# Regrouping the 512- and 256-column matmuls of a feed-forward block, and a 64-row contraction widened to 128 rows

## The chip, the cores and the metric

The kernel runs on one core of a Trainium2 chip. The metric is the device time of one execution in microseconds (us): the median of several runs. Beside it, one execution was taken with the hardware profiler, and its trace is what the rows below are copied from.

## The reference: what is computed

One decoder layer in float32 on 256 tokens of width 2048, then a final RMSNorm. Cut to its outline:

```python
h = rmsnorm(x, attn_norm_g)
proj = h @ w_in                         # split into latent q, latent kv, a shared rotary key, NSA q/k/v, gates
o_mla = mla_group(...)                  # 8 heads: s = q_nope.k_nope + q_rope.k_rope, causal softmax, p @ v
o_nsa = nsa_group(...)                  # 16 heads: compressed, selected and window branches, ALiBi, gates
x = x + concat(o_mla, o_nsa) @ w_o
h = rmsnorm(x, ffn_norm_g)
x = x + (silu(h @ w_gate) * (h @ w_up)) @ w_down      # D_FF = 5632
out = rmsnorm(x, final_norm_g)
```

Two places matter here. One is `h @ w_gate` and `h @ w_up`, which are 2048 x 5632 each. The other is the rotary term of the MLA scores, `q_rope . k_rope`, which contracts over 64 numbers per head.

## The kernel before, in words

**Numbers in two parts.** TensorE takes its operands in a reduced float32 form, so every operand is split into a high part (a rounded copy) and a low part (what the rounding left), and a product a·b is made as hi·hi + hi·lo + lo·hi. A weight chunk of 128 x 1024 float32 numbers is brought by a DMA (`wraw`), ScalarE writes its high part (`whi`, line 143) and VectorE its low part (`wlo`, line 145). `Stream` does this for all chunks in one fixed order: the DMA of a chunk is issued three chunks ahead and its split two ahead, in rings of three buffers. On SyncE's queue these DMAs stand in the order of the program, and each waits until its buffer is free.

**Order of the work.** TensorE's order is written out by hand in `program()`: the input projection, the NSA heads with other projections between them, the eight MLA heads with chunks of the output projection between them, the rest of the output projection, then the feed-forward block in two halves. The order on the other engines and queues comes from a scheduler that simulates the program.

**Gate and up.** A half is 22 tiles of 128 feed-forward columns. Each tile takes two weight chunks of `w_gate` and two of `w_up`; a chunk holds eight 128 x 128 pieces, one for each of eight groups of 128 inputs. The weights are the stationary operand, and the moving operand is `h2T`, the normed input transposed, with its high and low part side by side (2 x 256 columns). For each piece, `mmA` (line 212) issues two matmuls into one PSUM bank:

```python
nc.tensor.matmul(ps[0:hi.shape[1], :], hi, act, start=start, stop=False)                   # L214: 512 columns
nc.tensor.matmul(ps[0:hi.shape[1], 0:S], lo, act[:, 0, :], start=False, stop=stop)         # L215: 256 columns
```

`gate_up` (line 789) calls it for the eight pieces of a chunk, so on TensorE a 512-column matmul and a 256-column one take turns, each with a weight load of its own. There are 704 such pairs in each half (2 matrices, 22 tiles, 16 pieces), 1408 in all. When both chunks of a tile's `up` are done, `activate` (line 817) takes the two banks. Between and after the two halves, `down` multiplies by `w_down` with 512-column matmuls alone (lines 858 to 860), 528 in a half.

**The rotary key.** `rope_key` (line 576) makes the rotated key and splits it. Its high part `KRH` is stored twice, on partitions 0 to 63 and 64 to 127; so is its low part `KRL` (line 545, 128 x 256). A head's rotary query `qr[:, hh]` holds the query's high part on one half of the partitions and its low part on the other, so one matmul over 128 rows (line 615) gives (hi + lo)·KRH. The low part of the key is multiplied by the query's high half alone, with 64 rows (line 616):

```python
hr = slice(64 * hh, 64 * hh + 64)
nc.tensor.matmul(sv, qr[:, hh, q_], KRH[:, 0:n], start=False, stop=False)
nc.tensor.matmul(sv, qr[hr, hh, q_], KRL[hr, 0:n], start=False, stop=False)
```

`mla_scores` (line 605) does this twice in each of eight heads, for 128 and for 256 key columns, and follows it with the causal mask, a bf16 matmul by an identity (line 617). The NSA scores have a similar chain (lines 445 to 452), with a contraction over 70 rows, and the product of the NSA probabilities with the values (lines 516 and 517) is a run of two 512-column and two 256-column matmuls.

Of the kernel before, what the change touches and what calls it, by code (L numbers as in the profile page):

```python
# [9 lines left out]
F32 = mybir.dt.float32  # L10
F32R = mybir.dt.float32r
# [5 lines left out]
P = 128  # L17
S = 256
D = 2048
KD = D // P  # L20
# [140 lines left out]
def layer_kernel(ctx: ExitStack, tc: tile.TileContext, a: dict, out: bass.AP):  # L161
    nc = tc.nc
# [43 lines left out]
    def bcast_rows(dst, col, ps):  # L206
# [1 line left out]
        for t in range(2):  # L208
            nc.tensor.transpose(ps[:, t * P:(t + 1) * P], col[:, t:t + 1].to_broadcast([P, P]), ident)
        nc.scalar.copy(dst, ps[:, 0:S])  # L210

    def mmA(ps, hi, lo, act, start, stop):

        nc.tensor.matmul(ps[0:hi.shape[1], :], hi, act, start=start, stop=False)  # L214
        nc.tensor.matmul(ps[0:hi.shape[1], 0:S], lo, act[:, 0, :], start=False, stop=stop)  # L215

    def mm3(ps, hi, lo, act, start, stop):

# [4 lines left out]
    ps = ctx.enter_context(tc.tile_pool(name="ps", bufs=1, space=bass.MemoryType.PSUM))  # L223

    def bank(tag, name):
        return ps.tile([P, 512], F32, tag=tag, name=name, bufs=2 if tag in ("ds", "PT") else 1)
# [8 lines left out]
    ap = att.enter_context(tc.tile_pool(name="att", bufs=1))  # L235
# [32 lines left out]
    for k in range(KD):  # L268
        if k in (0, 1, 6, 10):
            c0 = (k + 3) // 4 * 4 if k < 6 else k + 2  # L270
            t = xcs[c0] = ap.tile([P, 4, S], F32, tag="xt", name=f"xt{c0}", bufs=2)
# [13 lines left out]
        if k in (5, 7, 9, 11):  # L285
            i = (k - 5) // 2
            t, xs = i // 2, slice(i % 2 * 1024, i % 2 * 1024 + 1024)
# [19 lines left out]
        hi, lo = W.get(("g1", k))  # L307
        st, sp = k == 0, k == KD - 1
# [74 lines left out]
    st = {}  # L383
# [158 lines left out]
    ckvT = ap.tile([P, 2, 2, S], F32R, tag="xt", name="ckvT", bufs=2)  # L542
    sqs = ap.tile([P, 2, S], F32, tag="xt", name="sqs", bufs=2)
    KRH = ap.tile([P, S], F32R, name="KRH")
    KRL = ap.tile([P, S], F32R, name="KRL")

    QR = oT[:, 4:8]

    def split(dh, dl, u, eng=nc.vector):
        nc.scalar.copy(dh, u)  # L550
        eng.tensor_sub(dl, u, dh.bitcast(F32))
# [24 lines left out]
    def rope_key():  # L576
        rp = bank("S0", "ps_ropek")
        nc.tensor.matmul(rp[0:64, 0:S], perm[0:64, 0:64], krg[0:64], start=True, stop=True)
        t = ap.tile([P, S], F32, tag="u", name="rt_k", bufs=2)
        nc.vector.tensor_mul(t[0:64], rp[0:64, 0:S], sinT[0:64])  # L580
        nc.gpsimd.tensor_mul(krg[0:64], krg[0:64], cosT[0:64])
        nc.gpsimd.tensor_add(t[0:64], krg[0:64], t[0:64])
        split(KRH[0:64], KRL[0:64], t[0:64])
        nc.scalar.copy(KRH[64:128], KRH[0:64].bitcast(F32))
        nc.vector.tensor_copy(KRL[64:128], KRL[0:64].bitcast(F32))

    def rope_queries(j):

# [16 lines left out]
    def mla_scores(m):  # L605
        hh, qn, qr = m % 2, st["qn", m], QR[:, m // 2]
        sb = bank("S0", f"ms_{m}")
        hr = slice(64 * hh, 64 * hh + 64)
        for t, sv in ((0, sb[:, 0:P]), (1, sb[:, P:384])):
            q_ = slice(t * P, (t + 1) * P)  # L610
            n = (t + 1) * P
            nc.tensor.matmul(sv, qn[:, 0, q_], KN[:, m, 0, 0:n], start=True, stop=False)
            nc.tensor.matmul(sv, qn[:, 0, q_], KN[:, m, 1, 0:n], start=False, stop=False)
            nc.tensor.matmul(sv, qn[:, 1, q_], KN[:, m, 0, 0:n], start=False, stop=False)
            nc.tensor.matmul(sv, qr[:, hh, q_], KRH[:, 0:n], start=False, stop=False)
            nc.tensor.matmul(sv, qr[hr, hh, q_], KRL[hr, 0:n], start=False, stop=False)
            nc.tensor.matmul(sv[:, n - P:n], identb, maskb[:, 0, :], start=False, stop=True)
        nm = ap.tile([P, 2, 2], F32, tag="nm", name=f"mnm{m}", bufs=2)
        ls = ap.tile([P, 2, 2], F32, tag="ls", name=f"mls{m}", bufs=2)
        nc.vector.tensor_reduce(nm[:, 0, 0:1], sb[:, 0:P], axis=AX.X, op=ALU.max)  # L620
        nc.vector.tensor_reduce(nm[:, 0, 1:2], sb[:, P:384], axis=AX.X, op=ALU.max)
        nc.vector.tensor_scalar(nm[:, 0, :], nm[:, 0, :], -MLA_SCALE, None, op0=ALU.mult)
        e = ap.tile([P, 768], F32, tag="e", name=f"me{m}", bufs=4)
        for t, c in ((0, slice(0, P)), (1, slice(P, 384))):
            nc.scalar.activation(e[:, c], sb[:, c], AF.Exp, bias=nm[:, 0, t:t + 1], scale=MLA_SCALE,
                                 accum_out=ls[:, 0, t:t + 1])
        nc.vector.reciprocal(ls[:, 0, :], ls[:, 0, :])
        for t, c in ((0, slice(0, P)), (1, slice(P, 384))):
            nc.vector.tensor_scalar(e[:, c], e[:, c], ls[:, 0, t:t + 1], None, op0=ALU.mult)
        st["me", m] = e  # L630
# [129 lines left out]
    for step in steps:  # L760
        op, args = step[0], step[1:]
        if op == "w":
            key = args[0]
            n = key[0]
            if n == "gate":
                break
            if n == "uk" and KN is None:
                big = hp.tile([P, KD, 2, S], F32R, tag="big", name="kn_v")
                KN = big[:, 0:8]
                VMM = big[:, 8:16].rearrange("p (t s a) h c -> p t s (a h c)", t=2, s=2)  # L770
            if n == "woM" and h2T is None:
                h2T = hp.tile([P, KD, 2, S], F32R, tag="big", name="h2T")
            w = W.get(key)
            if n in ("q", "cq", "ckv"):
                w_in_block(key, w)
            elif n in ("w1k", "w1v"):
                compress_hidden(n[2], key[1], w)
            elif n in ("woN", "woM"):
                w_o(key, w)
            else:  # L780
                {"uk": w_uk, "uv": w_uv, "uq": w_uq}[n](key[1], w)
        else:
            {"gates": do_gates, "rope_k": rope_key, "ck": compress_keys, "cv": compress_values,
             "ssq": latent_sum, "rb": latent_rows, "rope": rope_queries, "qk": nsa_scores, "t": nsa_transpose,
             "pv": nsa_pv, "tc": cmp_transpose, "pvc": cmp_pv, "mqk": mla_scores, "mt": mla_transpose,
             "mpv": mla_pv, "tp": transpose_x}[op](*args)


    def gate_up(key, w):
        n, f, j = key  # L790
        hi, lo = w
        if j == 0:
            st[n, f] = bank("ds" if n == "gate" else "PT", f"{n}{f}")
        for kk in range(8):
            k, c = 8 * j + kk, slice(kk * P, (kk + 1) * P)
            mmA(st[n, f], hi[:, c], lo[:, c], h2T[:, k], k == 0, k == KD - 1)

    W.share = 0
    while step[0] == "w":
        gate_up(step[1], W.get(step[1]))  # L800
        step = next(steps)
# [29 lines left out]
    for h in range(2):  # L831
        done = 0
        while done < NFH:
            step = next(steps)
            if step[0] == "rb2":
                bcast_rows(RB, rstd[:, 3, :], bank2("ps_rb2")[:, 0, :])
                continue
            n, f, j = step[1]
            gate_up(step[1], W.get(step[1]))
            if (n, j) == ("up", 1):  # L840
                activate(h, f - h * NFH)
                done += 1
# [179 lines left out]
```

## Time and profile before

| | us |
|---|---|
| median of 3 runs | 1085.76 |
| lowest, highest | 1083.0, 1086.45 |
| the profiled execution | 1083.73 |
| its span, first to last instruction | 1081.9 |
| TensorE busy in the span | 1059.7 |
| VectorE, ScalarE, GpSimd busy | 643.8, 563.3, 205.1 |

"Busy" TensorE counts modelled durations that overlap, so it can't be read as time at full rate. How fast the matmuls really follow each other is read from their start times: the difference between two starts, or a stretch between two starts divided by the number of matmuls in it.

### The profile page before, as it was taken

What the parts mean: (1) busy time and instruction counts of PE and PEld (TensorE: products, weight loads), DVE (VectorE), ACT (ScalarE), POOL (GpSimd) and SP (SyncE); (2) the same over time, 40 slices, a digit from 0 to 9 for tenths busy, and PEclk for the clock granted to TensorE, in tenths of its full rate; (3) what the DMA queues carried; (4) which work ended last, traced back from release to release, by engine and by line L of the source; (5) the groups of instructions that cost most, each with busy time, mean ns of one, the idle gap of its engine ahead of it and who ended that gap; (6) DMA issues with size and microseconds to landing.
All of it is one profiled execution on the core that took longest, in us unless ns stands there. A gap on an engine that the chain in (4) does not pass through costs nothing.

```text
span 1081.9 us, 16205 instructions
## 1 busy us (share of the span) xinstructions
PE 1059.7 (98%) x6102; PEld 926.0 (86%) x6102; DVE 643.8 (60%) x1017; ACT 563.3 (52%) x994; POOL 205.1 (19%) x206
## 2 busy tenths in 40 slices
PE   8999998999999999999999999999999999999996
PEld 8999997878888888888888888888888888888885
DVE  5568889885556555555555444455555555555554
ACT  6648887854455554544454333345444454444442
POOL 2234445533342100101010000001010010101110
PEclk9999999999999999999999999999999999999999
DMA  8845432334456555555565566655555555555653
GB/s 282 283 134 182 136 119 98 101 98 134 134 176 215 184 188 192 191 186 188 193 194 186 192 194 192 193 192 185 186 190 182 192 181 190 186 186 194 193 195 136
DMA packets 54831, 193.57 MB, mean 179 GB/s; under 512 B 6436, under 2 KB 6948, under 8 KB 54624
## 3 DMA queue, kind: packets, MB, share of 16 engines
q1 hardware_dynamic: 54288, 191.36, 53.9%
q0 software_dynamic: 464, 1.17, 0.3%
q8 instruction: 48, 0.79, 0.3%
q14 instruction: 31, 0.25, 0.1%
HBM read 190.41 MB, written 2.10 MB: 178 GB/s over the span
## 4 chain that ended last, share of the span: by engine, by line
PE 87%; DVE 4%; DMA 4%; ACT 2%; issue 2%; POOL 0%; SPq 0%; DVEq 0%; POOLq 0%; ACTq 0%
PE up L214 15%; PE gate L214 15%; PE gate L215 8%; PE up L215 8%; PE dn L859 7%; PE dn L858 7%; PE dn L860 7%; DMA wraw<-in_g_dram 2%; DMA wraw<-in_w_dram 1%; PE woM L747 1%; PE woM L748 1%; PE woM L749 1%; PE ps_q L219 1%; PE ps_q L220 1%; PE ps_q L221 1%
## 5 line engine op out<-in xcount | busy, mean ns | idle before, releaser
L145 DVE TENSOR_TENSOR wlo<-wraw,whi 128x1024 fp32r<-128x1024 f32 (+3 forms) x352 | 416.6, 1184 | 388.8 <-ACT whi L143 387.8
L143 ACT CAST whi<-wraw 128x1024 fp32r<-128x1024 f32 (+2 forms) x352 | 366.4, 1041 | 450.0 <-PE dn L860 125.1
L214 PE MATMUL gate<-h2T,whi 128*128 128x512 f32 x704 | 248.7, 395 | 0.0
L214 PE MATMUL up<-h2T,whi 128*128 128x512 f32 x704 | 248.5, 395 | 0.0
L215 PE MATMUL gate<-h2T,wlo 128*128 128x256 f32 x704 | 197.4, 280 | 0.0
L215 PE MATMUL up<-h2T,wlo 128*128 128x256 f32 x704 | 197.4, 280 | 0.0
L826 POOL TENSOR_TENSOR u<-t,RB 128x512 f32<-128x512 f32 x44 | 57.1, 1297 | 556.6 <-DVE t L825 556.6
L214 PEld LDWEIGHTS up<-h2T,whi 128*128 128x128 f32 x704 | 132.0, 187 | 31.0
L214 PEld LDWEIGHTS gate<-h2T,whi 128*128 128x128 f32 x704 | 132.0, 187 | 31.0
L858 PE MATMUL dn<-whi,aT 128*128 128x512 f32 x352 | 137.0, 389 | 0.0
L860 PE MATMUL dn<-whi,aT 128*128 128x512 f32 x352 | 137.0, 389 | 0.0
L859 PE MATMUL dn<-wlo,aT 128*128 128x512 f32 x352 | 137.0, 389 | 0.0
L215 PEld LDWEIGHTS gate<-h2T,wlo 128*128 128x128 f32 x704 | 133.0, 189 | 0.1
L215 PEld LDWEIGHTS up<-h2T,wlo 128*128 128x128 f32 x704 | 133.0, 189 | 0.0
L147 POOL TENSOR_TENSOR wlo<-wraw,whi 128x256 fp32r<-128x256 f32 x70 | 89.2, 1275 | 145.5 <-ACT whi L143 122.9
L858 PEld LDWEIGHTS dn<-whi,aT 128*128 128x128 f32 x352 | 66.1, 188 | 13.9
L860 PEld LDWEIGHTS dn<-whi,aT 128*128 128x128 f32 x352 | 66.1, 188 | 13.8
L859 PEld LDWEIGHTS dn<-wlo,aT 128*128 128x128 f32 x352 | 66.1, 188 | 13.5
L219 PE MATMUL ps_q<-hT,whi 128*128 128x256 f32 x128 | 38.1, 298 | 2.2 <-ACT RB L210 2.2
L221 PE MATMUL ps_q<-hT,wlo 128*128 128x256 f32 x128 | 36.9, 288 | 0.0
L220 PE MATMUL ps_q<-hT,whi 128*128 128x256 f32 x128 | 36.8, 288 | 0.0
L219 PEld LDWEIGHTS ps_q<-hT,whi 128*128 128x128 f32 x128 | 25.3, 198 | 2.9 <-ACT RB L210 2.5
(322 smaller groups left out, 1489.2 us busy)
## 6 DMA issues: line engine op xcount, KB each, us to landing
wraw<-in_w_dram SPq DMA_DIRECT2D x338, 512.0 KB, 3.5
wraw<-in_g_dram SPq DMA_DIRECT2D x14, 440.0 KB, 5.0
x<-in_x_dram SPq DMA_DIRECT2D x4, 512.0 KB, 5.9
out_dram<-x SPq DMA_DIRECT2D x8, 256.0 KB, 2.6
xt<-in_xT_dram SPq DMA_DIRECT2D x3, 512.0 KB, 6.2
gfin<-in_gfin_dram POOLq DMA_DIRECT2D x1, 1024.0 KB, 5.9
wraw<-in_g_dram SPq DMA_DIRECT2D x2, 256.0 KB, 4.0
wraw<-in_g_dram SPq DMA_DIRECT2D x2, 184.0 KB, 3.3
```

Of the source, the lines that this page charges most:

```text
L143: nc.scalar.copy(hi[:, c0:c1], raw[:, c0:c1])
L145: nc.vector.tensor_sub(lo[:, c0:c2], raw[:, c0:c2], hi[:, c0:c2].bitcast(F32))
L147: nc.gpsimd.tensor_sub(lo[:, c2:c1], raw[:, c2:c1], hi[:, c2:c1].bitcast(F32))
L214: nc.tensor.matmul(ps[0:hi.shape[1], :], hi, act, start=start, stop=False)
L215: nc.tensor.matmul(ps[0:hi.shape[1], 0:S], lo, act[:, 0, :], start=False, stop=stop)
L219: nc.tensor.matmul(ps, hi, act[:, 0, :], start=start, stop=False)
L220: nc.tensor.matmul(ps, hi, act[:, 1, :], start=False, stop=False)
L221: nc.tensor.matmul(ps, lo, act[:, 0, :], start=False, stop=stop)
L826: nc.gpsimd.tensor_mul(u, t2, RB[:, None, :].to_broadcast([P, 2, S]))
L858: nc.tensor.matmul(pts[t], h_, wh, start=f == 0, stop=False)
L859: nc.tensor.matmul(pts[t], h_, wl, start=False, stop=False)
L860: nc.tensor.matmul(pts[t], l_, wh, start=False, stop=f == NFH - 1)
```

## The change

In `gate_up` the pieces of a chunk are taken two at a time: the 512-column matmuls of both come first, then their two 256-column ones. The products, their operands and the bank are the same. In the MLA scores, `KRL` becomes a tile of 128 x 2 x 256 that is filled with zeros at the start of the program; slot 0 has the key's low part on partitions 0 to 63 and zeros on the others, slot 1 has zeros on 0 to 63 and the low part on 64 to 127. The matmul of line 616 takes the slot of its head and runs over all 128 rows, with zeros where the query's low part stands.

```diff
-    def mmA(ps, hi, lo, act, start, stop):
-
-        nc.tensor.matmul(ps[0:hi.shape[1], :], hi, act, start=start, stop=False)
-        nc.tensor.matmul(ps[0:hi.shape[1], 0:S], lo, act[:, 0, :], start=False, stop=stop)
...
-    KRL = ap.tile([P, S], F32R, name="KRL")
+
+    KRL = ap.tile([P, 2, S], F32R, name="KRL")
+    nc.gpsimd.memset(KRL.bitcast(F32), 0.0)
...
-        split(KRH[0:64], KRL[0:64], t[0:64])
+        split(KRH[0:64], KRL[0:64, 0, :], t[0:64])
         nc.scalar.copy(KRH[64:128], KRH[0:64].bitcast(F32))
-        nc.vector.tensor_copy(KRL[64:128], KRL[0:64].bitcast(F32))
+        nc.vector.tensor_copy(KRL[64:128, 1, :], KRL[0:64, 0, :].bitcast(F32))
...
-        hr = slice(64 * hh, 64 * hh + 64)
...
-            nc.tensor.matmul(sv, qr[hr, hh, q_], KRL[hr, 0:n], start=False, stop=False)
+            nc.tensor.matmul(sv, qr[:, hh, q_], KRL[:, hh, 0:n], start=False, stop=False)
...
-        for kk in range(8):
-            k, c = 8 * j + kk, slice(kk * P, (kk + 1) * P)
-            mmA(st[n, f], hi[:, c], lo[:, c], h2T[:, k], k == 0, k == KD - 1)
+        pt = st[n, f]
+        for k2 in range(0, 8, 2):
+            for kk in (k2, k2 + 1):
+                k = 8 * j + kk
+                nc.tensor.matmul(pt, hi[:, kk * P:(kk + 1) * P], h2T[:, k], start=k == 0, stop=False)
+            for kk in (k2, k2 + 1):
+                k = 8 * j + kk
+                nc.tensor.matmul(pt[:, 0:S], lo[:, kk * P:(kk + 1) * P], h2T[:, k, 0, :], start=False, stop=k == KD - 1)
```

On TensorE, the first chunk of the first gate tile stood like this before:

```order
L748 MATMUL woM_4097<-wlo_4150,oT 128x512
L749 MATMUL woM_4097<-whi_4149,oT 128x512
L214 MATMUL gate_4197<-h2T,whi_4168 128x512
L215 MATMUL gate_4197<-h2T,wlo_4169 128x256
L214 MATMUL gate_4197<-h2T,whi_4168 128x512
L215 MATMUL gate_4197<-h2T,wlo_4169 128x256
L214 MATMUL gate_4197<-h2T,whi_4168 128x512
L215 MATMUL gate_4197<-h2T,wlo_4169 128x256
```

and stands like this now (x2 means two alike in a row):

```order
L794 MATMUL gate_4198<-h2T,whi_4169 128x512 x2
L797 MATMUL gate_4198<-h2T,wlo_4170 128x256 x2
L794 MATMUL gate_4198<-h2T,whi_4169 128x512 x2
L797 MATMUL gate_4198<-h2T,wlo_4170 128x256 x2
L794 MATMUL gate_4198<-h2T,whi_4169 128x512 x2
```

The matmuls are the same ones; in each four, the second and the third have changed places.

The scheduler's order of the other engines moves as well. On SyncE's queue, in the input projection's first microseconds (`xt` is the transposed input in pieces of four groups, `wraw` the weight chunks):

```order
 L122 DMA wraw_115<-in_g_dram 128x880
 L122 DMA wraw_155<-in_g_dram 128x880
-L280 DMA xt_150<-in_xT_dram 128x1024
 L122 DMA wraw_184<-in_g_dram 128x880
+L275 DMA xt_150<-in_xT_dram 128x1024
 L122 DMA wraw_215<-in_g_dram 128x880
```

The second piece of the transposed input is now issued behind the fifth weight chunk. ScalarE and VectorE split that chunk before they scale that input piece, where it was the other way round. On GpSimd one memset, that of `KRL`, stands behind the other memsets of the start. In the first half, ScalarE and VectorE now split a tile's result (`aT`) before they read the next tile's gate bank, where it was the other way round.

## Rows read from the trace of the kernel before

**Rows 1.** The page: TensorE's busy time, and the chain that ended last, by line.

```profile
PE 1059.7 (98%) x6102; PEld 926.0 (86%) x6102; DVE 643.8 (60%) x1017; ACT 563.3 (52%) x994; POOL 205.1 (19%) x206
...
PE up L214 15%; PE gate L214 15%; PE gate L215 8%; PE up L215 8%; PE dn L859 7%; PE dn L858 7%; PE dn L860 7%; DMA wraw<-in_g_dram 2%; DMA wraw<-in_w_dram 1%; PE woM L747 1%; PE woM L748 1%; PE woM L749 1%; PE ps_q L219 1%; PE ps_q L220 1%; PE ps_q L221 1%
```

**Rows 2.** Timeline of PE: start, duration (us), instruction, [idle before]; where feed-forward stretches meet.

```profile
352.07 0.48 PE L214 MATMUL gate<-h2T,whi 128*128 128x512 f32 x1
...
585.12 0.39 PE L858 MATMUL dn<-whi,aT 128*128 128x512 f32 x1
...
953.57 0.40 PE L858 MATMUL dn<-whi,aT 128*128 128x512 f32 x1
```

**Rows 3.** Timeline of PE: the first gate matmuls of the second half.

```profile
704.84 0.39 PE L214 MATMUL gate<-h2T,whi 128*128 128x512 f32 x1
705.07 0.28 PE L215 MATMUL gate<-h2T,wlo 128*128 128x256 f32 x1
705.18 0.40 PE L214 MATMUL gate<-h2T,whi 128*128 128x512 f32 x1
```

**Rows 4.** Timeline of PE: first and last of 15 256-column matmuls in a row.

```profile
162.01 0.28 PE L219 MATMUL ps_q<-hT,whi 128*128 128x256 f32 x1
...
163.69 0.28 PE L221 MATMUL ps_q<-hT,wlo 128*128 128x256 f32 x1
```

**Rows 5.** Timeline of PE: NSA probabilities by values, behind the run of rows 4.

```profile
163.81 0.39 PE L516 MATMUL o<-ph,V 128*128 128x512 f32 x1
164.04 0.40 PE L517 MATMUL o<-pl,V 128*128 128x512 f32 x1
164.27 0.29 PE L516 MATMUL o<-ph,V 128*128 128x256 f32 x1
164.40 0.28 PE L517 MATMUL o<-pl,V 128*128 128x256 f32 x1
164.52 0.40 PE L529 MATMUL o<-PCT,VCS 80*128 80x512 f32 x1
```

**Rows 6.** Timeline of PE: score matmuls of the third MLA head (rows*columns of weights first).

```profile
239.56 0.27 PE L614 MATMUL ms<-kn_v,qn 128*128 128x128 f32 x1
239.67 0.27 PE L615 MATMUL ms<-KRH,oT 128*128 128x128 f32 x1
239.87 0.32 PE L616 MATMUL ms<-KRL,oT 64*128 64x128 f32 x1
240.13 0.23 PE L617 MATMUL ms<-maskb,identb 128*128 128x128 bf16 x1
...
240.60 0.28 PE L615 MATMUL ms<-KRH,oT 128*128 128x256 f32 x1
240.81 0.38 PE L616 MATMUL ms<-KRL,oT 64*128 64x256 f32 x1
241.12 0.23 PE L617 MATMUL ms<-maskb,identb 128*128 128x128 bf16 x1
```

**Rows 7.** Timeline of PE: an NSA score's 70-row matmul and the bf16 mask behind it.

```profile
160.69 0.28 PE L451 MATMUL s<-KA,qa 70*128 70x256 f32 x1
160.82 0.29 PE L452 MATMUL s<-maskb,identb 128*128 128x256 bf16 x1
```

**Rows 8.** Busy time by window: window, its length, each engine's busy us, granted clock.

```profile
205.00:240.00 35.00, 33.70 (x205) 27.89 (x203) 29.46 (x66) 21.27 (x51) 11.67 (x11) 1.00 0.30 98
```

**Rows 9.** Timeline of several engines in the first microseconds.

```profile
2.55 0.54 POOL L329 MEMSET bl_k<- 128x512 f32 x1
...
7.16 0.43 SPq L280 DMA_DIRECT2D xt<-in_xT_dram  x1
9.58 0.33 SPq L122 DMA_DIRECT2D wraw<-in_g_dram  x1
...
13.40 1.71 ACT L303 ACTIVATE hT<-xt,gcols 128x256 fp32r<-128x256 f32 x4 [0.33 <-DMA xt<-in_xT_dram]
...
17.07 0.28 PE L219 MATMUL ps_kc<-hT,whi 128*128 128x256 f32 x1
```

## The prediction

> **What bounds the kernel now.** I read the page first. TensorE is busy for 98% of the span, and the chain that ended last runs through its matmuls: gate and up alone hold 46% of it, the large ones 30% and the small ones 16% [rows 1]. A change in the spacing of these matmuls therefore goes straight into the time, unless another engine is late; so all that matters is how far apart matmuls start, which the timeline of PE shows.
>
> Three spacings are worked out from start times. (a) `down` alone: 528 matmuls of 512 columns between 585.12 and 704.84 [rows 2, 3], 226.7 ns each. Half of that, 113.3 ns, is what 256 columns would take at the same rate. (b) 256-column matmuls alone: 14 steps in 1.68 us [rows 4], 120 ns each, so a short matmul costs some 7 ns over its share. Each has a weight load of its own, which must fit beside one short matmul. (c) Gate and up, a pair of 512 and 256 columns: the first half has 672 pairs from 352.07 to 585.12 [rows 2], 346.8 ns each. That is (a) + (b), 226.7 + 120 = 346.7. The second half has 704 pairs from 704.84 to 953.57 [rows 2, 3], 353.3 ns each: the same instructions, 6.5 ns more for every pair. The reader is to see that the alternating order has two steady rhythms, and that the slower one costs 704 x 6.5 = 4.6 us here. The second half came out of `down` with the first pair at 0.34 us (704.84 to 705.18), so nothing was late when it fell into the slow rhythm. Over both halves the mean is (233.05 + 248.73) / 1376 = 350.1 ns a pair, 700 ns for two pairs. The 32 pairs ahead of 352.07 stand between transposes and are taken at this mean.
>
> **The change, gate and up.** No matmul, load, byte or wait is added. Two pairs (large, small, large, small) become a group (large, large, small, small); there are 704 groups. In a group the second large matmul's load and the first small one's load lie under large matmuls; the loads of the second small one and of the next large one lie under short ones. That is two loads under short matmuls in a group, as before in two pairs. What should change is the rhythm: each group has a 512 to 512 step, which in (a) takes 226.7 with nothing left over.
> - Lower bound: everything hidden, 3 x 226.7 = 680 ns a group. Gain (700 - 680) x 704 = 14.1 us.
> - Upper bound: the one stretch of the trace with just this order, two 512s and two 256s on the NSA values, takes 164.52 - 163.81 = 0.71 us [rows 5]. It stands once, behind a run of short matmuls, and its moving operand lies in two pieces. Loss (710 - 700) x 704 = 7.0 us.
> - Taken: 226.7 + 226.7 + 120 + 120 = 693.4 ns, (a) and (b) added up, because that sum is what the first half's pairs hold for 233 us, and a long steady stretch says more of 704 groups than a single four. Gain: (353.3 - 346.7) x 704 = 4.6 us in the second half, nothing in the first, 0.1 us in the 32 pairs: **4.7 us**.
>
> One rule of the Trainium skill speaks against this part. Its page "TensorE: Matmul & The Clock Gate", section LDWEIGHTS, has a load of 128 columns at 106.7 ns, and its section Back-to-back issue gap has 256 columns at 109 ns: by it every load hides under a short matmul too, either order takes the same, and the sum would hold the rotary part alone. The trace does not agree fully: 120 ns against 113.3 [rows 4, 2, 3]. I keep the rule as a rival.
>
> **The change, rotary key.** 16 matmuls lose their 64-row shape. In the third head the step from the 128-row matmul to the 64-row one is 0.20 us where two 128-row ones are 0.11 apart, and the next step, to the mask, is 0.26; for 256 columns the two are 0.21 and 0.31 [rows 6]. Each is long enough for the matmul ahead to run dry before the next weights are loaded. With 128 rows the steps become 0.11 (239.56 to 239.67) and 0.11 for 128 columns; for 256 columns 0.12 by (b), and 0.13 for the step into a bf16 mask, which a 70-row contraction has without such a gap [rows 7]. Saved in a head: (0.20 - 0.11) + (0.26 - 0.11) + (0.21 - 0.12) + (0.31 - 0.13) = 0.51 us, and 4.1 us in eight. The first heads lie in a stretch in which TensorE waits (33.70 us busy of 35, at a granted clock of 1.00 [rows 8]), so one head's gain is put down as lost in waits: **3.6 us** from seven. The bounds are 0 (the steps come from something else) and 4.1.
>
> The Trainium skill has a rule for either side of this. Its page "TensorEngine Tiling (Array Packing)", Key Properties, says that changing the tiling mode drains TensorE, by which the gain is as above. The Trainium skill's "TensorE: Matmul & The Clock Gate", Step-by-step, says that a load takes no less for fewer rows, by which alone the widening would be worth nothing. The steps of 0.20 and 0.26 agree with the first.
>
> **What is moved beside it, costed at nothing.** The second input piece's DMA goes from 7.16 us to just behind the weight DMA at 9.58, so it is issued some 2.8 us later; its first user on ScalarE started at 13.40, and the input group that it brings is first multiplied at 17.07 [rows 9]. Its high part takes 0.43 us (a quarter of 1.71), the low part about as much (an estimate): 2.8 us of slack against 2.8. Cost 0; without cover, at most a few tenths. The memset on GpSimd (0.54 us, as for `bl_k` [rows 9]) stands ahead of a one-column copy that this DMA waits for, and is done long before 9.58. The exchanged readings of the gate banks have a whole tile's time before the bank is used again. A chunk's high part is released by its last large matmul, now one small matmul earlier; its low part at the same place.
>
> **Sum.** 1083.73 (the profiled execution, span 1081.9) - 4.7 - 3.6 = **1075.4 us**. The median of the runs shown is 2.0 us above the profiled execution; more tiles in the slow rhythm could account for that, and it would go with it. It takes some 0.3%, 3.3 us, to tell a run of this kernel from no change.
>
> **The rivals.**
> 1. *The order is indifferent*: the excess belongs to the number of short matmuls, and the rhythm is picked by chance at the start of a half. For it: both rhythms occur with the same code. Against it: the slow one lasts a whole half, so it is no chance from tile to tile. With the present mean the gate and up part is worth nothing, 1083.73 - 3.6 = 1080.1; with 353.3 in both halves the first loses 672 x 6.5 = 4.4 us, 1084.5. The rule of the Trainium skill on load and gap would have it so, without saying which rhythm.
> 2. *The large pair covers more*: it lets the weight path run ahead, so that only one short matmul of a group pays its 7 ns: 226.7 x 2 + 113.3 + 120 = 686.7, a gain of 9.4 us, 1070.7; with all hidden 1066.0. For it: the first small matmul behind `down` was followed after 0.11 us [rows 3]. Against it: it may just hand the delay on.
> 3. *Slower*: two loads in a row under short matmuls leave the weight path behind, and the next large one starts late each time, as in the NSA values: 0.71 us a group gives 1083.73 + 7.0 - 3.6 = 1087.1, and 0.73, if each of those steps is 0.005 worse than shown, 1101. It is slower from 710 ns on. For it: the one example. Against it: long runs of short matmuls hold 120.
> 4. *The rotary gain does not show* (the gap is not the 64 rows', or VectorE's softmax is late instead): 1083.73 - 4.7 = 1079.0.
>
> **How the numbers follow.** Forecast 41%; rival 1 29%, of which a third at 1080.1 counts as faster and the rest as no change; rival 2 17%; rival 3 6%; rival 4 7%. Faster: 0.41 + 0.17 + 0.07 + 0.09 = 0.74; same 0.20; slower 0.06. The range, 1069.5 to 1084.5, leaves out rival 3, the end of rival 2 with all hidden, and a little of rival 1. The forecast's own range is 1074 to 1078.
>
> **What would show it.** In the changed profile: 704.8 us shifted earlier by about 3.6 us and not more; each half of gate and up with groups of 693 ns, some 244 us for 704 pairs; no step of 0.2 us around the line that multiplies by `KRL`; the 64*128 shape gone. Wrong would be: groups at 700 or 707 ns (rival 1), at 687 or less (rival 2), or a wait of TensorE for ScalarE, VectorE or a DMA that is not there now.

## The result and the profile after

| | before | changed |
|---|---|---|
| median of 4 runs, us | 1085.32 | 1077.12 |
| lowest, highest | 1083.0, 1086.45 | 1076.86, 1078.08 |
| the profiled execution | 1083.73 | 1077.04 |
| its span | 1081.9 | 1075.3 |

The changed kernel is faster: a ratio of 0.9934, 95% interval 0.9921 to 0.9947, a small gain of 0.7%. The profiled executions differ by 6.7 us, the medians by 8.2. (The kernel before has one run more here than in its first table.)

On the page of the changed kernel TensorE is still what bounds it, and gate and up still hold 46% of the chain, now under lines 794 and 797 [rows 1].

```profile
PE 1052.0 (98%) x6102; PEld 920.3 (86%) x6102; DVE 645.7 (60%) x1017; ACT 562.9 (52%) x994; POOL 205.5 (19%) x207
...
PE up L794 15%; PE gate L794 15%; PE up L797 8%; PE gate L797 8%; PE dn L860 7%; PE dn L861 7%; PE dn L859 7%; DMA wraw<-in_g_dram 2%; PE ps_q L214 1%; PE woM L743 1%; PE woM L745 1%; PE woM L744 1%; PE ps_q L215 1%; PE ps_q L216 1%; DVE wlo L145 1%
```

The timeline of PE in the changed kernel (start, duration in us, instruction; x2 joins two alike) has these rows at the joints that rows 2, 3 and 6 show of the kernel before: the last matmul of the NSA scores, the third MLA head, the first gate tile, the gate tile behind the transposes, the start of the second half and each start of `down`.

```profile
203.00 0.29 PE L447 MATMUL s<-maskb,identb 128*128 128x256 bf16 x1
...
237.62 0.27 PE L610 MATMUL ms<-kn_v,qn 128*128 128x128 f32 x1
237.73 0.27 PE L611 MATMUL ms<-KRH,oT 128*128 128x128 f32 x1
237.84 0.27 PE L612 MATMUL ms<-KRL,oT 128*128 128x128 f32 x1
237.95 0.23 PE L613 MATMUL ms<-maskb,identb 128*128 128x128 bf16 x1
237.99 0.36 PE L608 MATMUL ms<-kn_v,qn 128*128 128x256 f32 x1
238.20 0.28 PE L609 MATMUL ms<-kn_v,qn 128*128 128x256 f32 x1
...
238.43 0.28 PE L611 MATMUL ms<-KRH,oT 128*128 128x256 f32 x1
238.55 0.28 PE L612 MATMUL ms<-KRL,oT 128*128 128x256 f32 x1
238.67 0.23 PE L613 MATMUL ms<-maskb,identb 128*128 128x128 bf16 x1
...
334.87 0.62 PE L794 MATMUL gate<-h2T,whi 128*128 128x512 f32 x2
...
347.02 0.48 PE L794 MATMUL gate<-h2T,whi 128*128 128x512 f32 x1
...
581.19 0.40 PE L859 MATMUL dn<-whi,aT 128*128 128x512 f32 x1
...
700.88 0.62 PE L794 MATMUL gate<-h2T,whi 128*128 128x512 f32 x2
...
946.10 0.40 PE L859 MATMUL dn<-whi,aT 128*128 128x512 f32 x1
```

The last matmul of the NSA scores and the first gate matmul of the kernel before, on the same view:

```profile
204.59 0.29 PE L452 MATMUL s<-maskb,identb 128*128 128x256 bf16 x1
...
339.86 0.39 PE L214 MATMUL gate<-h2T,whi 128*128 128x512 f32 x1
```

From starts alone, the span divides into six stretches:

| stretch | before, us | changed, us | difference |
|---|---|---|---|
| start to the last matmul of the NSA scores | 204.59 | 203.00 | -1.59 |
| from there to the first gate matmul (the eight MLA heads and the output projection) | 135.27 | 131.87 | -3.40 |
| gate and up, first half | 245.26 | 246.32 | +1.06 |
| `down`, first half | 119.72 | 119.69 | -0.03 |
| gate and up, second half | 248.73 | 245.22 | -3.51 |
| the rest | 128.4 | 129.2 | +0.8 |
| span | 1081.9 | 1075.3 | -6.7 |

The last two differences are taken before rounding.

The reader is to see three things. The long steps around `KRL` are gone: four steps of 0.11, 0.11, 0.12 and 0.12 us stand where rows 6 had 0.20, 0.26, 0.21 and 0.31. A group of four takes 245.22 / 352 = 696.6 ns in the second half, and both halves now have one and the same spacing: 348.5 ns a pair from 347.02 to 581.19 (672 pairs), 348.3 from 700.88 to 946.10 (704), where it was 346.8 and 353.3 [rows 2, 3]. So the second half gained and **the first half lost 1.06 us**. And two stretches in which the prediction put nothing moved, by -1.59 and +0.8.

In the first of these two, the granted clock fell at different places in the two executions. One place is in the NSA queries, where TensorE waits for the copy of `RB` (line 210). The timeline of PE before ([idle before] in brackets):

```profile
49.25 0.39 PE L219 MATMUL ps_q<-hT,whi 128*128 128x256 f32 x1 [2.24 <-ACT RB L210]
...
49.72 0.41 PE L219 MATMUL ps_q<-hT,whi 128*128 128x256 f32 x1
...
52.92 0.36 PE L219 MATMUL ps_q<-hT,whi 128*128 128x256 f32 x1
```

and changed:

```profile
48.87 0.38 PE L214 MATMUL ps_q<-hT,whi 128*128 128x256 f32 x1 [1.64 <-ACT RB L210]
```

TensorE's busy time by window (window, its length, busy us and instructions, granted clock, DMA share, GB/s), before:

```profile
49.60:53.00 3.40, 3.40 (x19) 0.51 0.74 261
189.40:192.80 3.40, 3.40 (x10) 0.53 0.29 81
```

Changed:

```profile
49.60:53.00 3.40, 3.40 (x31) 1.00 0.86 240
70.20:73.60 3.40, 3.40 (x19) 0.57 0.66 210
```

Before, the wait of 2.24 us was followed by a granted clock of 0.51, the level of 1.2 GHz, and 15 matmuls of 256 columns started 0.213 us apart (3.20 us from 49.72 to 52.92) instead of 0.12, which is 1.4 us more. In the changed kernel the clock stayed at 1.00 there, the 2.4 GHz level, and fell near 70 us instead; the kernel before had a second fall near 190 us, which the changed one had not. One fall more in the kernel before, at some 1.4 us (an estimate from the first), is about the 1.59; the waits of this stretch differ too and were not taken apart. Whether this belongs to the change is asked of the repeated runs below.

The second is a wait at the end, where TensorE waits 0.6 us for the split of a chunk of `w_down`. Behind it stands ScalarE, which splits the last chunks, on its timeline in the changed kernel:

```profile
1053.77 2.00 ACT L143 CAST whi<-wraw 128x1024 fp32r<-128x1024 f32 x2 [3.04 <-DMA wraw<-in_w_dram]
```

The same cast in the kernel before:

```profile
1060.30 2.00 ACT L143 CAST whi<-wraw 128x1024 fp32r<-128x1024 f32 x2 [2.05 <-DMA wraw<-in_w_dram]
```

ScalarE waits 3.04 us for the DMA there against 2.05, and only the longer wait reaches TensorE.

### The profile page after: what moved, and what is told of

Read it like the earlier page. It is cut to its first block, busy times and chain, and to the rows that moved or that the text cites. A ratio compares the mean times of both kernels' runs of the same rounds, so it can differ in the third digit from the quotient of the medians.

```text
span 1075.3 us, 16205 instructions
## 1 busy us (share of the span) xinstructions
PE 1052.0 (98%) x6102; PEld 920.3 (86%) x6102; DVE 645.7 (60%) x1017; ACT 562.9 (52%) x994; POOL 205.5 (19%) x207
## 4 chain that ended last, share of the span: by engine, by line
PE 88%; DVE 4%; DMA 4%; ACT 2%; issue 1%; SPq 0%; POOL 0%; DVEq 0%; POOLq 0%; ACTq 0%
PE up L794 15%; PE gate L794 15%; PE up L797 8%; PE gate L797 8%; PE dn L860 7%; PE dn L861 7%; PE dn L859 7%; DMA wraw<-in_g_dram 2%; PE ps_q L214 1%; PE woM L743 1%; PE woM L745 1%; PE woM L744 1%; PE ps_q L215 1%; PE ps_q L216 1%; DVE wlo L145 1%
## 5 line engine op out<-in xcount | busy, mean ns | idle before, releaser
L794 PE MATMUL gate<-h2T,whi 128*128 128x512 f32 x704 | 221.2, 396 | 0.0
L794 PE MATMUL up<-h2T,whi 128*128 128x512 f32 x704 | 221.1, 395 | 0.0
L797 PE MATMUL gate<-h2T,wlo 128*128 128x256 f32 x704 | 138.3, 278 | 0.0
L797 PE MATMUL up<-h2T,wlo 128*128 128x256 f32 x704 | 138.3, 278 | 0.0
L794 PEld LDWEIGHTS gate<-h2T,whi 128*128 128x128 f32 x704 | 107.3, 189 | 0.2
L794 PEld LDWEIGHTS up<-h2T,whi 128*128 128x128 f32 x704 | 107.2, 189 | 0.0
L743 PE MATMUL woN<-whi,oT 128*128 128x512 f32 x64 | 26.6, 416 | 0.4 <-ACT oT L547 0.4
```

What stands on the lines that cost most here:

```text
L794: nc.tensor.matmul(pt, hi[:, kk * P:(kk + 1) * P], h2T[:, k], start=k == 0, stop=False)
L797: nc.tensor.matmul(pt[:, 0:S], lo[:, kk * P:(kk + 1) * P], h2T[:, k, 0, :], start=False, stop=k == KD - 1)
```

## The experiments

Medians are of 5 or 6 runs each (12 for the kernel before run again) against 10 to 17 of the kernel before on the same chip; the one with 384 columns was run once. The rhythms are worked out as above: from the gate tile after the 32 first pairs to the first `down` matmul (672 pairs), and from the second half's first gate matmul to its first `down` (704 pairs).

### Each part alone

The rotary part alone, with `gate_up` as before:

```diff
-    KRL = ap.tile([P, S], F32R, name="KRL")
+    KRL = ap.tile([P, 2, S], F32R, name="KRL")
...
-            nc.tensor.matmul(sv, qr[hr, hh, q_], KRL[hr, 0:n], start=False, stop=False)
+            nc.tensor.matmul(sv, qr[:, hh, q_], KRL[:, hh, 0:n], start=False, stop=False)
```

> The rotary part alone, gate and up in the old order. Theory (the 64-row shape makes the steps of 0.20 to 0.31 us): a head's score matmuls end 0.51 us sooner, the last MLA head ends about 3 us earlier against the NSA stage, and the time is 3 to 4 us (0.3 to 0.4%) below the kernel before. Gate and up keep the two rhythms of the kernel before: 346.8 ns a pair in the first half, 353.3 in the second. Rival (the drain is not the 64 rows, or VectorE takes its place): no change of the time.

Measured: 1079.12 us, ratio 0.9952 [0.9936, 0.9968]. Its timeline of PE at the joints:

```profile
348.81 0.48 PE L214 MATMUL gate<-h2T,whi 128*128 128x512 f32 x1
...
581.86 0.39 PE L858 MATMUL dn<-whi,aT 128*128 128x512 f32 x1
...
701.58 0.39 PE L214 MATMUL gate<-h2T,whi 128*128 128x512 f32 x1
...
950.31 0.40 PE L858 MATMUL dn<-whi,aT 128*128 128x512 f32 x1
```

That is 233.05 / 672 = 346.8 ns and 248.73 / 704 = 353.3: to the digit the two rhythms of [rows 2, 3], in the same halves. From the last matmul of the NSA scores (204.73) to the first gate matmul (336.60) it takes 131.87 us, as the changed kernel does: the 3.40 us belong to the rotary part alone. The medians differ by 5.8 us, more than the 3 to 4 expected, with 3.5 to 6.9 in the interval.

The regrouping alone, with the 64-row `KRL`:

```diff
-            mmA(st[n, f], hi[:, c], lo[:, c], h2T[:, k], k == 0, k == KD - 1)
+        for k2 in range(0, 8, 2):
...
```

> The grouping alone, 64-row matmuls kept. Theory: both halves run at 697 ns for two pairs as in the changed kernel, so the first half loses 1.1 us against 346.8 a pair and the second gains 3.5 against 353.3: 2 to 3 us (0.2 to 0.3%) below the kernel before. Rival (the grouping does nothing, the rhythm of a half is chance): a half at 693 or 707.

Measured: 1080.64 us, 0.9967 [0.9951, 0.9984]; 348.5 and 348.3 ns a pair. The rows around `KRL` are those of [rows 6] again:

```profile
238.05 0.28 PE L615 MATMUL ms<-KRH,oT 128*128 128x256 f32 x1
238.26 0.38 PE L616 MATMUL ms<-KRL,oT 64*128 64x256 f32 x1
238.57 0.23 PE L617 MATMUL ms<-maskb,identb 128*128 128x128 bf16 x1
```

The stretch from the last matmul of the NSA scores (202.03) to the first gate matmul (337.30) is 135.27 us again. So the steps of 0.21 and 0.31 us and the 3.40 us come and go with the 64-row shape, the spacing in gate and up with the grouping, and on TensorE's timeline the two parts don't touch each other. The gains of the two, 0.48% and 0.33%, add up to 0.81%, and to the change's 0.66% within their intervals.

### What a short matmul costs

Two readings of the 7 ns that a 256-column matmul takes beyond half of a 512-column one were set against each other: that its weight load does not fit beside it (A), or that the change of size between neighbours costs it (B). The first test takes all eight pieces of a chunk as one group, eight large matmuls, then eight small:

```diff
-        for k2 in range(0, 8, 2):
-            for kk in (k2, k2 + 1):
+        for k2 in range(0, 8, 8):
+            for kk in range(k2, k2 + 8):
```

> The changed kernel with all eight large matmuls of a chunk first and then its eight small ones. Theory A (a weight load under a short matmul costs 7 ns, whatever stands around it): 8 x 226.7 + 8 x 120 and some 25 ns until the large ones have settled, 347 to 350 ns a pair, so within 2 us of the changed kernel. Theory B (the excess comes with each change of length, 8.4 ns each in groups of two): 2.1 ns a pair remain over 340.1, 342 ns a pair, 8 to 9 us below the changed kernel.

Measured: 1079.79 us, 0.9955 [0.9939, 0.9972]. 234.73 / 672 = 349.3 and 245.79 / 704 = 349.1 ns a pair, with a quarter of the changes of size. B had 342 and falls as it was put; A had 347 to 350, which holds. But a change of size is not free either. The timeline of PE in the second half:

```profile
721.49 2.00 PE L794 MATMUL up<-h2T,whi 128*128 128x512 f32 x8
723.33 1.12 PE L797 MATMUL up<-h2T,wlo 128*128 128x256 f32 x8
724.28 2.00 PE L794 MATMUL gate<-h2T,whi 128*128 128x512 f32 x8
```

Eight large matmuls behind small ones take 1.84 us, 230 ns each where a long run has 226.7, and eight small ones behind large ones 0.95 us, 119 ns each where a long run has 120. What this order pays over the sum of the two, some 2.4 ns a pair, lies in the large matmuls behind the small ones.

The second test gives the small matmul, in the alternating order, 16 columns more:

```diff
-        nc.tensor.matmul(ps[0:hi.shape[1], 0:S], lo, act[:, 0, :], start=False, stop=stop)
+        flat = act.rearrange("p a c -> p (a c)")
+        nc.tensor.matmul(ps[0:hi.shape[1], 0:272], lo, flat[:, 0:272], start=False, stop=stop)
```

> The rotary part, gate and up in the old alternating order, but the small matmul streams 272 columns instead of 256 (16 tokens also get low times low, which the result sums in). 272 columns take 120.4 ns at the rate of the large ones. Theory A (a weight load needs some 120 ns and a 256-column matmul is a little too short for it): the load now fits, and a pair takes 347.1 in both halves, with no slow rhythm: the second half 4.4 us shorter than in the kernel before, the whole 1 to 2 us below the changed kernel. Theory B (change of length): 7 ns longer columns on top of either rhythm, 354 to 360 a pair, 8 us above the changed kernel.

Measured: 1091.88 us, 1.0065 [1.005, 1.0081]. 239.76 / 672 = 356.8 and 253.43 / 704 = 360.0 ns a pair; A had the added columns hidden by the load, and they are not: each half is 6.7 to 10 ns a pair above its old rhythm. (B's 354 to 360 takes in both values; it is the groups of eight that speak against B. The whole time rose by 7.0 us over the kernel before, which neither had.) With A fallen as well, a third reading (C) was formed: every matmul takes its columns at 2.4 GHz and a fixed 13.3 ns. It fits what was there, at a granted clock of 1.00: 512 / 2.4 + 13.3 = 226.7 [rows 2, 3] and 256 / 2.4 + 13.3 = 120.0 [rows 4], and was put to a size that the kernel does not have, 384 columns for both matmuls of a pair:

```diff
+            c1 = 512 if k == 0 else 384
+            nc.tensor.matmul(pt[:, 0:c1], hi[:, c], act[:, 0:c1], start=k == 0, stop=False)
+            nc.tensor.matmul(pt[:, 128:512], lo[:, c], act[:, 128:512], start=False, stop=k == KD - 1)
```

> The rotary part, and both matmuls of a gate or up piece take 384 columns (the high weights leave out the low part of 128 tokens, the low weights take in columns that the result doesn't need; the first piece of a tile keeps its 512). No weight load lies under a matmul that is too short for it. Theory C (a matmul costs its columns at 2.4 GHz and a fixed 13.3 ns: 226.7 for 512, 120 for 256, 126.7 for 272): 173.3 ns a matmul, 346.7 a pair. Theory A (226.7/512 a column, and short ones pay for their load): 170.0 a matmul, 340.0 a pair.

Its timeline of PE, first and last of 24 such matmuls in a row:

```profile
823.91 0.33 PE L798 MATMUL up<-h2T,whi 128*128 128x384 f32 x1
...
827.89 0.33 PE L799 MATMUL up<-h2T,wlo 128*128 128x384 f32 x1
```

23 steps in 3.98 us are 173.0 ns; C gives 384 / 2.4 + 13.3 = 173.3, and A 170.0. Over the whole second half (704.56 to 951.56) a pair takes 350.8 ns, where C, with the 512 columns of each tile's first piece, gives 350.0. A whole execution took 1081.66 us. So three sizes lie on one line. The sum for a pair, 226.7 + 120.0 = 346.7 ns, 693.3 for a group, is called the floor below: no half of any run with these two sizes held less. The line does not go down to 128 columns, where it would give 66.7 ns: the score matmuls shown above start 0.11 us apart. And each matmul here brings a weight load of its own, so whether the 13.3 ns belong to the matmul or to the change of weights was not tested.

### The entry into the second half

If the old order's two rhythms are both steady, what comes just before a half may choose between them. The first half's good stretch begins behind two transposes (line 209). The kernel before shows more of it, ahead of that stretch (timeline of PE):

```profile
340.91 0.40 PE L214 MATMUL gate<-h2T,whi 128*128 128x512 f32 x1
...
345.15 0.40 PE L214 MATMUL up<-h2T,whi 128*128 128x512 f32 x1
345.39 0.28 PE L215 MATMUL up<-h2T,wlo 128*128 128x256 f32 x1
345.51 1.03 PE L661 MATMUL tp<-cst,x 128*128 128x128 f32 x8
...
346.73 0.40 PE L214 MATMUL gate<-h2T,whi 128*128 128x512 f32 x1
...
351.59 0.39 PE L214 MATMUL up<-h2T,whi 128*128 128x512 f32 x1
```

The first 16 pairs of the first half come behind 512-column matmuls of the output projection and go at the slow rhythm: 12 pairs in 4.24 us, 353.3 ns each. Then come eight transposes, and behind them 14 pairs take 4.86 us, 347 each. So the slow rhythm is not the second half's own. The kernel of this experiment has the rotary part, the alternating order, and two like transposes of `rstd`, whose result is not used, ahead of the second half:

```diff
+        if h == 1:
+            kick = bank2("ps_kick")[:, 0, :]
+            for t in range(2):
+                nc.tensor.transpose(kick[:, t * P:(t + 1) * P], rstd[:, 3, t:t + 1].to_broadcast([P, P]), ident)
```

> The rotary part, gate and up in the old alternating order, and two 128-column transposes (of a vector that is there, into a bank that nobody reads) ahead of the second half's first gate matmul. Theory (a stretch keeps the rhythm that it is entered with: behind transposes 346.8 ns a pair, behind 512-column matmuls 353.3): the second half now runs at 346.8, 4.6 us less than with the rotary part alone, for 0.2 us of transposes; 1 to 2.5 us below the changed kernel. Rival (the second half is slow because of its place, its buffers or its DMAs): 353.3 as before, the time of the rotary part alone.

Measured: 1075.31 us, 0.9923 [0.9906, 0.994].

```profile
700.40 0.38 PE L836 MATMUL ps_kick<-cst,rstd 128*128 128x128 f32 x2
700.53 0.47 PE L214 MATMUL gate<-h2T,whi 128*128 128x512 f32 x1
...
944.67 0.39 PE L862 MATMUL dn<-whi,aT 128*128 128x512 f32 x1
```

244.14 / 704 = 346.8 ns: the second half is in the faster rhythm, for two matmuls that take 0.13 us. What stands at the entry sets the rhythm, and it is held for 704 pairs. Whether it needs transposes, or any short break in the stream would do, was not tried.

### The mask's load

In the changed kernel the step behind the bf16 mask is uneven: 0.04 us to the next matmul and then 0.21. The kernel with the two transposes, run with mask and identity in the reduced float32 form, asks whether that costs anything.

```diff
-    identb = cp.tile([P, P], BF16, name="identb")
-    maskb = cp.tile([P, 2, P], BF16, name="maskb")
+    identb = cp.tile([P, P], F32R, name="identb")
+    maskb = cp.tile([P, 2, P], F32R, name="maskb")
```

> As the kernel with the two transposes, and the mask and its identity in reduced float32 instead of bf16, in the MLA and the NSA scores. Theory (the steps of 0.04 and 0.20 us behind a bf16 mask are a weight load that is not brought forward): they become 0.06 and 0.12, 0.06 to 0.07 us saved at each of 16 masks in the MLA heads and a little in the NSA ones, 1 to 2 us in all, less what VectorE hides. Rival: the steps add up to the same, no change.

Measured: 1075.55 us, 0.9922 [0.9907, 0.9936], as without the edit. On the timeline of PE:

```profile
238.18 0.27 PE L616 MATMUL ms<-KRL,oT 128*128 128x128 f32 x1
238.29 0.28 PE L617 MATMUL ms<-maskb,identb 128*128 128x128 f32 x1
238.41 0.33 PE L612 MATMUL ms<-kn_v,qn 128*128 128x256 f32 x1
238.58 0.28 PE L613 MATMUL ms<-kn_v,qn 128*128 128x256 f32 x1
```

The three steps from `KRL` on are 0.11 + 0.12 + 0.17 = 0.40 us, against 0.11 + 0.04 + 0.21 = 0.36 in the changed kernel above (237.84 to 238.20). The stretch from the NSA scores to the first gate matmul is 132.1 us here and 131.9 without the edit. The 1 to 2 us that were expected did not come: the bf16 mask is no loss.

### The three kernels again, on one chip

The kernel before, the changed one and the one with the two transposes were run once more, unchanged, side by side.

> The kernel before, once more with a profile. Theory (a half keeps the rhythm that its entry gives): 346.8 and 353.3 ns a pair in the two halves again, to 0.1. Rival (rhythms come by chance): other values. Open beside it: whether TensorE's wait for the normalising rows near 47 us is again 2 us or more and the matmuls behind it run at a granted clock below 1, some 1.7 us, which would be part of what the first comparison of profiles showed.

> The changed kernel on the same chip as the others of this call. Theory: 348.4 ns a pair in both halves, 3.0 to 4.5 us for the rotary part; 0.6 to 0.7% below the kernel before.

> The kernel with the two transposes on the same chip as the changed kernel. Theory: 346.8 ns a pair in both halves against 348.4, so 1408 x 1.6 = 2.3 us less than the changed kernel and 0.2 us back for the transposes. Rival: the medians cannot be told apart.

Measured: 1085.1 us, ratio to itself 1.0006 [0.9995, 1.0018]; the changed kernel 1077.44, 0.9936 [0.9924, 0.9949]; the one with transposes 1077.14, 0.9938 [0.9926, 0.995]. By their times the last two can't be told apart. In gate and up they can, by TensorE's busy time in the windows of both halves; the changed kernel, then the one with transposes:

```profile
337.47:583.79 246.32, 246.32 (x1419) 1.00 0.59 192
703.48:948.70 245.22, 245.22 (x1410) 1.00 0.59 189
```

```profile
338.72:583.98 245.26, 245.26 (x1419) 1.00 0.59 193
703.71:947.98 244.27, 244.27 (x1411) 1.00 0.59 190
```

491.54 against 489.53 us, 2.0 us less, and the changed kernel's two halves take what they took in its first profile, to the hundredth. The kernel before showed 346.8 and 353.3 ns again. The stretch from the last matmul of the NSA scores to the first gate matmul is 135.27 us in it again (204.08 to 339.35) and 131.88 in the changed kernel (205.59 to 337.47). What differs from run to run is the early part. The window from 40 to 60 us in the second profile of the kernel before:

```profile
40.00:60.00 20.00, 18.39 (x149) 1.00 0.61 194
```

and in that of the changed kernel:

```profile
40.00:60.00 20.00, 18.16 (x138) 0.91 0.61 199
```

The granted clock in three such windows of each profile:

| | 40 to 60 us | 60 to 80 us | 180 to 200 us |
|---|---|---|---|
| before, first profile | 0.91 | 1.00 | 0.91 |
| before, second | 1.00 | 0.91 | 0.91 |
| changed, first profile | 1.00 | 0.91 | 1.00 |
| changed, second | 0.91 | 0.83 | 0.91 |

Either kernel has the first window at 1.00 in one execution and at 0.91 in the other, and the number of falls differs between two executions of the changed kernel. So the slow clock in the first stretch of the table is no work of the change. Nor is the stall at the end: the second profile of the kernel before has one too (ScalarE's cast waited 3.10 us for its DMA, and TensorE 0.7 for the split).

## Why the prediction was right, and where it was not

The forecast of 1075.4 us was 1.6 below the profiled 1077.04 and 1.7 below the median; the sign and both mechanisms hold. But its two terms came out differently.

**Rotary key: right.** A head was to save 0.51 us by its four steps; they add up to 0.98 us in [rows 6] and to 0.46 now, 0.52. All eight lie between the last matmul of the NSA scores and the first gate matmul, and that stretch is 3.40 us shorter, against 3.6 forecast from seven heads; it was the same to 0.02 us in every profile with either shape of `KRL` and the bf16 mask. From the third head's first score matmul on (239.56 and 237.62) 3.05 us are saved, 0.51 in each of six heads. The first two gave 0.35 of their 1.02: TensorE's wait for VectorE's `pl` between them grew from 0.24 us to 0.78. The forecast put that loss down at one head, and it was 1.3. That the gap belongs to the 64 rows is shown from both sides, by each part alone. The rule weighed in the prediction, of the Trainium skill's "TensorEngine Tiling (Array Packing)", Key Properties, that a change of tiling mode drains TensorE, agrees; its price here is (0.20 - 0.11) + (0.26 - 0.11) = 0.24 us for 128 columns and 0.28 for 256, in and out.

**Gate and up: right in sign, the term mis-sized.** The forecast was 4.6 us in the second half and nothing in the first; measured were 3.51 gained and 1.06 lost, 2.45 in all. The step that failed is "227 + 227 + 120 + 120": 693.4 ns a group was taken for what the new order would hold, because the first half held it. It is the floor, as defined above, and the new order runs 3.3 ns above it in the second half and 3.6 in the first. The old order had 346.8 in one half and 353.3 in the other, so the change swapped a mix of a good and a bad rhythm for one in between. The term was mis-sized by 2.25 us, 4.7 against 2.45. The prediction's own rows warned of it: the order that was being replaced had reached the floor over 233 us, and nothing in them showed the new one there.

**The lower bound and rival 2 had no ground.** Both took half of 226.7, 113.3 ns, as a short matmul with all hidden, and read the other 7 ns as a load that does not fit. Single steps of 0.11 us behind a large matmul do occur [rows 3], but no long run held them; with 13.3 ns for each matmul of 256, 384 and 512 columns alike there is no ground for 113.3 as a steady spacing, nor for 680 or 686.7 ns a group. Reading (A) was that one; the 272 columns and the 173.0 ns of 384 speak against it. By the rate of the Trainium skill's "TensorE: Matmul & The Clock Gate", LDWEIGHTS, a load of 128 columns takes 106.7 ns (an estimate from its columns / 1.2), less than a short matmul's 120, and nothing here speaks against that; by its Back-to-back issue gap 256 columns take 109 ns (an estimate), and 120 were measured.

**The other rivals.** The order is not indifferent (rival 1: 700 or 707 ns, measured 697), and it is not slower (rival 3: from 710 on). The upper bound rests on a misreading: the four of [rows 5] does not stand once. The trace before has it 16 times, and 12 of these without a wait inside. The ten behind 256-column matmuls took 0.71 us; the two behind 512-column ones took 0.70 (as from 222.53 to 223.23), which is the nearer to a steady group's 0.697.

**What was costed at nothing.** The second input piece's DMA was issued at 10.03 us (9.9 by the estimate), its scaling began at 15.02, 1.6 later than before, and the group it brings was multiplied at 16.98 (17.07 before) without a wait: the slack covered it.

**Luck in the sum.** 8.3 us were forecast from the profiled execution and 6.7 came. Of these, the two parts gave 5.85 (3.40 and 2.45); the stretch ahead of the MLA heads added 1.59 and the end took 0.8, both of them of the run and not of the change. So the parts fell 8.3 - 5.85 = 2.45 us short of the forecast, and the run's own differences covered 0.8 of it. The changed kernel's two profiles have spans of 1075.3 and 1078.0 us, so an agreement to 1.7 us in one of them says less than the terms do. The prediction's sign, a second half that starts some 3.6 us earlier, came out at 3.96, but as 1.59 + 3.40 + 0.03 - 1.06, and so says little as well.

**What stays open.** What inside TensorE makes the alternating order settle at 346.8 or at 353.3, and why large matmuls behind small ones start late by what the grouped orders pay, was not found; that the entry decides in the first case is shown, and what it is about the transposes is not. Why a chunk near the end of `w_down` lands late in most of the profiled executions was not tried. The median of the kernel before stands above both of its profiled runs, and no profile was taken of such a run.

## What to carry to other kernels

Before regrouping a pair of matmuls, take the spacing of each size in a long run of its own; if the present order already holds their sum somewhere, that sum is the best seen so far, and the question is why the other stretches miss it. Here two transposes at the entry brought the second half to it, as the new order did not (2.0 us less in gate and up, too little to tell the whole times apart). Read a steady stretch by the difference of starts over hundreds of matmuls, and compare each half or stage apart: the total hid a loss of 1.06 us in the first. And a contraction over 64 rows is not cheaper if it stands between full ones: padding with zeros to 128 rows took 0.51 us off each of six heads, and less where TensorE had another wait to come.

## What the runs showed of the hardware that was not expected

- In this reduced float32 form a matmul's spacing at the 2.4 GHz level is its columns at that clock and 13.3 ns: 226.7 ns for 512, 173.0 measured (173.3) for 384, 120.0 for 256. At 128 columns it is not: 0.11 us in the MLA scores.
- One instruction stream has two steady spacings, 346.8 and 353.3 ns a pair; two transposes of 0.13 us ahead of it brought the faster for 704 pairs. With 272 columns the pair lies above the floor of 353.3 by 3.5 ns in one half and by 6.7 in the other.
- At the 1.2 GHz level the fixed part is gone: 256 columns took 3.20 us / 15 = 213.3 ns, which is 256 / 1.2, and 512 columns, from 189.92 to 192.48 us of the kernel before, 2.56 us / 6 = 426.7 ns, which is 512 / 1.2. The Trainium skill's "TensorE: Matmul & The Clock Gate", section Wait — 56ns, not 53.3ns?, has a fixed cost of each matmul that shows only at 2.4 GHz; the runs agree in kind, but it puts 2.5 ns where 13.3 were measured here.
- After a wait of 2.24 us the granted clock was 0.51 from 49.6 to 53.0 us, and 15 matmuls of 256 columns stood 0.213 us apart; after one of 1.64 us at the same place, in the changed kernel, it stayed at 1.00 there and was 0.57 from 70.2 to 73.6 us.
